# RWKV time mixing on one core: unit 1 loaded as bf16 in two halves through the casting queue, weights loaded by channel halves, and half of the second weight scaled on ScalarE

## The chip, the core and the metric

The kernel runs on one core of one Trainium2 chip. A core has a matrix engine (TensorE, PE in the profile), a vector engine (VectorE, DVE), a scalar engine (ScalarE, ACT), GpSimd (POOL) and SyncE (SP), which here only starts DMAs. Each engine works through its own instructions in order and waits on semaphores for the others. The metric is the device time of one execution in microseconds; lower is better. The median of five runs of the kernel before is 201.86 us (201.51 to 202.05).

## What is computed

Three mixes of each row of `x` with the row before it are the start of the reference; the one for `k` doesn't reach the output, and the kernel leaves it out.

```python
x_prev[:, 1:, :] = x[:, :-1, :]
xv = x * time_mix_v + x_prev * (1 - time_mix_v)
xr = x * time_mix_r + x_prev * (1 - time_mix_r)
v = xv.reshape(-1, d_model) @ value_weight
r = xr.reshape(-1, d_model) @ receptance_weight
r_sigmoid = 1.0 / (1.0 + np.exp(-r))
out = (r_sigmoid * v).reshape(-1, d_model) @ output_weight
```

`x` is 16 x 2048 x 256 in float32, each weight 256 x 256, the output has the shape of `x`.

## The kernel before

**Tiling.** The 16 x 2048 rows are cut into 64 units of 512 rows; four units make a batch row `b`. In a unit each of 128 partitions holds `UJ = 4` consecutive rows. The 256 channels are two groups `ko` of 128 (`KO = 2`). For the projections the channels must lie on the partitions, so each unit is transposed into a tile `xt` (called `xt_first` in the profile for the first two batch rows): as a rule 8 transposes on TensorE into a PSUM tile `ps_t`, and a copy by ScalarE. A slot of `xt` holds the rows with one index `j`; "previous row" is then the slot before, and a slot copy (`wrap_slots`, L431 and L432) fills the first slot of a unit.

**The algebra.** The mix is written as `time_mix * (x + c * x_prev)` with `c = 1/time_mix - 1`. The factor `time_mix` is scaled into the weights, once at the start: `w_bf[:, 0]` is the receptance weight and `w_bf[:, 1]` the value weight, each with two channel groups `ko`. The mix per unit is then a scaling (L262 on VectorE, L272 on GpSimd, or L519 on ScalarE) and an addition (L284 on VectorE). The factors are `tms` (time_mix), `c_sb` (c) and `tm_prev` (1 - time_mix); `coefficients` computes them on VectorE from a small transposed tile (L174 to L187).

**Unit by unit.** For each unit `g`: the receptance projection (4 matmuls of 512 columns), the sigmoid on ScalarE (L539), the value projection (4 matmuls), the product on VectorE (L585), 8 output matmuls (L316), a copy by ScalarE (L350) and a store by SP. Between them stand the mixes of the next units and the transposes of units some way ahead. The order on each engine is the order in which the program issues the instructions: it is written out by hand (`manual_schedule`), and waits come from the tiles.

**The start.** This is where the change lies. TensorE warms up on zeros. Meanwhile:

- SP loads, in this order: unit 0 as float32 into `x_unit[:, 0]`, in two halves of two rows each, the second half (`h = 1`) first; the receptance weight into `w_f32[:, 0]`; unit 1 as float32 into `x_unit[:, 1]`, by halves; the value weight into `w_f32[:, 1]` (L130, L136, L140). In the profile `x_unit` has the name `o_sb`, from its pool.
- GpSimd makes the DMAs that cast from float32 to bf16 on the way. The first ones bring unit 2 and unit 3 into `x_first` (L149); a one-column copy ahead of them (L147) reads the loaded receptance weight and writes into `x_first`, so that the casts are issued only after that weight has landed. Behind them come the output weight (L150), four units of batch row 1 (L108) and, later, whole batch rows (L114).
- TensorE transposes unit 0 as float32 (L234), with the coefficients' transpose in between, and ScalarE copies it out (L239, L243).
- VectorE computes the coefficients, `tms`, `tm_prev`, then `c_sb`; then it scales the receptance weight to `w_prev` (two instructions, L459) and the first channel group to `w_bf[:, 0, 0]` (L466). ScalarE scales the second, `w_bf[:, 0, 1]` (L469). VectorE then makes unit 0's value mix and scales both channel groups of the value weight (L475).
- Unit 0's receptance is projected without a mix, from `xt` and shifted `xt`, with `w_prev` and `w_bf[:, 0]` (`project_unmixed`, L306), in two output halves `mo`. Between the two stand unit 1's transposes, from float32 (L210, called by `advance(1)`), with their two copies by ScalarE (L220). The first sigmoid follows.

These are the lines around that point, in the order in which they are issued:

```python
project_unmixed(ps_r, 0)
advance(1)
project_unmixed(ps_r, 1)
wrap_slots(pieces(1)[0])
scale(pieces(1)[0])
last = add(pieces(1)[0])
```

Of the kernel before, what the change touches and what calls it, by code (L numbers as in the profile page):

```python
# [8 lines left out]
FP32 = mybir.dt.float32  # L9
BF16 = mybir.dt.bfloat16  # L10
ALU = mybir.AluOpType
ACT = mybir.ActivationFunctionType
# [3 lines left out]
def kernel(  # L16
# [38 lines left out]
    H = UJ // 2  # L55
# [11 lines left out]
    consts = ctx.enter_context(tc.tile_pool(name="consts", bufs=1))  # L67
# [4 lines left out]
    opool = ctx.enter_context(tc.tile_pool(name="opool", bufs=3))  # L72
    ps_t_pool = ctx.enter_context(tc.tile_pool(name="ps_t", bufs=2, space=bass.MemoryType.PSUM))
# [9 lines left out]
    x_bf = {}  # L83
    xt = {}
    mix = {}
    o_sb = {}
# [4 lines left out]
    ident_f = consts.tile([P, P], FP32)  # L91
    make_identity(nc, ident_f)
    ident = consts.tile([P, P], BF16)
# [5 lines left out]
    def unit_rows(t, b, e, n=1):  # L99

        return t[b, e * TU : (e + n) * TU, :].rearrange("(e p j) d -> p e j d", p=P, j=UJ)
# [15 lines left out]
            for j in (0, J // 2)  # L117
        ]

    x_unit = opool.tile([P, 2, UJ, D], FP32, name="o_sb")  # L120
    tm_rows = consts.tile([2 * KO, P], FP32)
    w_f32 = consts.tile([P, 2, KO, D], FP32)
    for m, tm in enumerate([time_mix_r, time_mix_v]):
        nc.scalar.dma_start(
            out=tm_rows[m * KO : (m + 1) * KO, :], in_=tm.rearrange("(ko p) -> ko p", p=P)
        )

    def load_halves(e):
        for h in (1, 0):
            nc.sync.dma_start(  # L130
                out=x_unit[:, e, h * H : (h + 1) * H],
                in_=unit_rows(x, 0, e)[:, 0, h * H : (h + 1) * H, :],
            )

    load_halves(0)
    nc.sync.dma_start(  # L136
        out=w_f32[:, 0], in_=receptance_weight.rearrange("(ko p) n -> p ko n", p=P)
    )
    load_halves(1)
    nc.sync.dma_start(out=w_f32[:, 1], in_=value_weight.rearrange("(ko p) n -> p ko n", p=P))  # L140
    sig0 = consts.tile([P, 1], BF16)
    nc.scalar.activation(out=sig0, in_=zeros[:, 0:1], func=ACT.Sigmoid)
    w_bf = consts.tile([P, 2, KO, D], BF16)
    w_prev = consts.tile([P, KO, D], BF16)
    wo_bf = consts.tile([P, KO, D], BF16)
    x_first = consts.tile([P, 2, UJ, D], BF16)
    nc.gpsimd.tensor_copy(out=x_first[:, 0, 0, 0:1], in_=w_f32[:, 0, 0, 0:1])  # L147
    for e in (2, 3):
        nc.gpsimd.dma_start(out=x_first[:, e - 2], in_=unit_rows(x, 0, e)[:, 0])  # L149
# [22 lines left out]
    def coefficients():  # L172
        ps = ps_o_pool.tile([P, 2, KO], FP32, name="psum_o")
        nc.tensor.transpose(  # L174
            out=ps.rearrange("p m k -> p (m k)"), in_=tm_rows, identity=ident_f[: 2 * KO, : 2 * KO]
        )
        tm = consts.tile([P, 2, KO], FP32)
        nc.vector.tensor_copy(out=tm, in_=ps)
        nc.vector.tensor_scalar(
            out=tms, in0=tm, scalar1=0.0, scalar2=1e-30, op0=ALU.is_equal, op1=ALU.mult  # L180
        )
        nc.vector.tensor_tensor(out=tms, in0=tms, in1=tm, op=ALU.add)
        nc.vector.tensor_scalar(
            out=tm_prev, in0=tm, scalar1=-1.0, scalar2=1.0, op0=ALU.mult, op1=ALU.add
        )
# [12 lines left out]
    def transposes(i):  # L198

        b, e = divmod(i, UB)  # L200
        if b > 0 and e == 0:
            new_xt(b)
        if b >= BYUNIT:
            e = (e - 1) % UB
        j0 = 1 + e * UJ + (e if b < BYUNIT else 0)
        if b < BYUNIT or e == UB - 1:
            late_copies.append((b, e))

        def one(ps, jj, ko, src, idn):
            nc.tensor.transpose(  # L210
                out=ps[:, jj], in_=src[:, jj, ko * P : (ko + 1) * P], identity=idn
            )

        if i == 1:
            for h in (1, 0):
                ps = ps_t_pool.tile([P, H, KO, P], FP32, name="ps_t")
                for jj in range(H):
                    for ko in range(KO):
                        one(ps[:, :, ko], jj, ko, x_unit[:, i, h * H : (h + 1) * H], ident_f)
                nc.scalar.copy(out=xt[b][:, j0 + h * H : j0 + (h + 1) * H], in_=ps)  # L220
            return
        ps = ps_t_pool.tile([P, UJ, KO, P], BF16, name="ps_t")
        src = x_first[:, e - 2] if b == 0 else x_bf[b][:, e * UJ : (e + 1) * UJ, :]
        for jj in range(UJ):
            for ko in range(KO):
                one(ps[:, :, ko], jj, ko, src, ident)
        nc.scalar.copy(out=xt[b][:, j0 : j0 + UJ], in_=ps)  # L227

    def first_transposes():
        def part(lo, n, pool, name):  # L230
            ps = pool.tile([P, n, KO, P], FP32, name=name)
            for jj in range(n):
                for ko in range(KO):
                    nc.tensor.transpose(  # L234
                        out=ps[:, jj, ko],
                        in_=x_unit[:, 0, lo + jj, ko * P : (ko + 1) * P],
                        identity=ident_f,
                    )
# [20 lines left out]
    def scale(piece, kos=(0, 1)):  # L259
        b, m, _, _ = piece  # L260
        for ko in kos:
            nc.vector.tensor_scalar(  # L262
                out=mixed(piece)[:, :, ko],
                in0=xt[b][:, slots(piece), ko],
                scalar1=c_sb[:, m, ko : ko + 1],
                scalar2=None,
                op0=ALU.mult,
            )
# [189 lines left out]
    for ko in range(KO):  # L458
        nc.vector.tensor_scalar(  # L459
            out=w_prev[:, ko, :],  # L460
            in0=w_f32[:, 0, ko, :],
            scalar1=tm_prev[:, 0, ko : ko + 1],
            scalar2=None,
            op0=ALU.mult,
        )
# [3 lines left out]
    nc.scalar.activation(  # L469
        out=w_bf[:, 0, 1, :], in_=w_f32[:, 0, 1, :], func=ACT.Copy, scale=tms[:, 0, 1:2]  # L470
    )
    scale(pieces(0)[1])
    add(pieces(0)[1])
    for ko in range(KO):
        nc.vector.tensor_scalar(  # L475
            out=w_bf[:, 1, ko, :],
            in0=w_f32[:, 1, ko, :],
            scalar1=tms[:, 1, ko : ko + 1],
            scalar2=None,
            op0=ALU.mult,  # L480
        )
    warm_up(WARM2)


# [42 lines left out]
    for g in range(NU - 1):  # L527
# [106 lines left out]
```

## Time and profile before

| | |
|---|---|
| median of five runs | 201.86 us (201.51 to 202.05) |
| profiled execution | 201.84 us |
| its span, first to last instruction | 200.1 us |
| busy TensorE | 195.0 us (97%) |
| busy VectorE | 185.7 us (93%) |
| busy ScalarE | 181.0 us (90%) |
| busy GpSimd | 83.5 us (42%) |
| granted TensorE clock | 1.0 |
| read from HBM, written | 34.34 MB, 33.55 MB |

How to read it: the four compute engines are busy at the same time, and a unit takes about 3.05 us in the middle of the run (from one value projection at 45.74 us to the next at 48.79). The share of busy time is a mean over the run. In the first 20 us the picture is another one, since engines wait for first data. The loads of the start, from the view of DMA issues (KB are those that are written, the last column is the median time from issue to landing):

```profile
o_sb<-in_x_dram SPq DMA_DIRECT2D x4, 256.0 KB, 3.9
x_bf<-in_x_dram POOLq DMA_DIRECT2D x4, 256.0 KB, 7.1
x_first<-in_x_dram POOLq DMA_DIRECT2D x2, 256.0 KB, 4.2
w_f<-n_receptance_weight_dram SPq DMA_DIRECT2D x1, 256.0 KB, 4.1
w_f<-in_value_weight_dram SPq DMA_DIRECT2D x1, 256.0 KB, 5.0
wo_bf<-in_output_weight_dram POOLq DMA_DIRECT2D x1, 128.0 KB, 5.4
```

### The profile page before, as it was taken

What the parts mean: (1) busy time and instruction counts of PE and PEld (TensorE: products, weight loads), DVE (VectorE), ACT (ScalarE), POOL (GpSimd) and SP (SyncE); (2) the same over time, 40 slices, a digit from 0 to 9 for tenths busy, and PEclk for the clock granted to TensorE, in tenths of its full rate; (3) what the DMA queues carried; (4) which work ended last, traced back from release to release, by engine and by line L of the source; (5) the groups of instructions that cost most, each with busy time, mean ns of one, the idle gap of its engine ahead of it and who ended that gap; (6) DMA issues with size and microseconds to landing.
All of it is one profiled execution on the core that took longest, in us unless ns stands there. A gap on an engine that the chain in (4) does not pass through costs nothing.

```text
span 200.1 us, 3885 instructions
## 1 busy us (share of the span) xinstructions
PE 195.0 (97%) x1419; PEld 124.9 (62%) x1419; DVE 185.7 (93%) x292; ACT 181.0 (90%) x204; POOL 83.5 (42%) x115
## 2 busy tenths in 40 slices
PE   8999999999999999999999999999999999999993
PEld 7555676666666666666666666655656665655671
DVE  1899999999999999899999999999999999999982
ACT  3799899999999999999999999899999999999982
POOL 1756562452543543425443444443344444444200
PEclk9999999999999999999999999999999999999999
DMA  5899999999999999999999999999999999999675
GB/s 165 233 170 213 216 279 274 280 279 275 289 309 305 288 272 288 288 277 288 283 278 301 303 404 309 313 189 208 291 263 406 356 205 244 416 421 414 277 310 214
DMA packets 32442, 57.00 MB, mean 285 GB/s; under 512 B 21796, under 2 KB 23080, under 8 KB 28456
## 3 DMA queue, kind: packets, MB, share of 16 engines
q1 hardware_dynamic: 28208, 40.24, 58.6%
q0 software_dynamic: 4064, 16.39, 40.9%
q8 instruction: 11, 0.18, 0.3%
q10 hardware_dynamic: 152, 0.13, 0.2%
q14 instruction: 7, 0.06, 0.1%
HBM read 34.34 MB, written 33.55 MB: 339 GB/s over the span
## 4 chain that ended last, share of the span: by engine, by line
PE 85%; DVE 7%; issue 3%; ACT 2%; POOL 1%; DVEq 0%
PE psum_v L292 25%; PE psum_o L316 24%; PE psum_r L292 24%; PE ps_t L210 8%; DVE z_sb L585 2%; DVE mix L284 2%; DVE mix L262 2%; PE ps_t L156 1%; PE ps_t L316 1%; PE psum_r L306 1%; ACT mix L519 1%; ACT s_sb L539 1%; ACT xt L227 1%; PE psum_r L234 0%; PE ps_t L292 0%
## 5 line engine op out<-in xcount | busy, mean ns | idle before, releaser
L272 POOL TENSOR_SCALAR mix<-xt,c_sb 128x1024 bf16<-128x1024 bf16 (+1 forms) x55 | 61.0, 1109 | 93.0 <-DVE mix L284 84.5
L585 DVE TENSOR_TENSOR z_sb<-s_sb,psum_v 128x1024 bf16<-128x1024 bf16 (+1 forms) x64 | 76.7, 1199 | 3.1 <-PE psum_v L292 1.4
L284 DVE TENSOR_TENSOR mix<-mix,xt 128x1024 bf16<-128x1024 bf16 x112 | 77.6, 702 | 1.9 <-DVE mix L262 0.5
L292 PEld LDWEIGHTS <-w_bf 128*128 128x128 bf16 x516 | 48.7, 98 | 38.7 <-DVE mix L284 0.9
L539 ACT ACTIVATE s_sb<-psum_r 128x1024 bf16<-128x1024 f32 x63 | 65.3, 1037 | 3.7 <-PE psum_r L292 2.7
L350 ACT COPY o_sb<-psum_o 128x1024 f32<-128x1024 f32 x60 | 61.5, 1025 | 6.8 <-PE psum_o L316 6.7
L292 PE MATMUL psum_v<-mix,w_bf 128*128 128x512 bf16 (+1 forms) x256 | 65.3, 377 | 0.2
L292 PE MATMUL psum_r<-mix,w_bf 128*128 128x512 bf16 (+1 forms) x252 | 64.3, 377 | 0.2
L316 PE MATMUL psum_o<-wo_bf,z_sb 128*128 128x256 bf16 x486 | 63.2, 272 | 0.0
L316 PEld LDWEIGHTS <-z_sb 128*128 128x128 bf16 x512 | 49.8, 98 | 20.4 <-issue 1.4
L227 ACT COPY xt<-ps_t 128x1024 bf16<-128x1024 bf16 x36 | 36.9, 1040 | 0.0
L210 PEld LDWEIGHTS <-x_bf 128*128 128x128 bf16 x320 | 20.9, 98 | 8.7 <-DMA x_bf<-in_x_dram 0.4
L210 PE MATMUL ps_t<-ident,x_bf 128*128 128x128 bf16 x320 | 23.9, 219 | 0.0
L262 DVE TENSOR_SCALAR mix<-xt,c_sb 128x1024 bf16<-128x1024 bf16 (+1 forms) x49 | 22.1, 459 | 0.0
L519 ACT ACTIVATE mix<-xt,c_sb 128x1024 bf16<-128x1024 bf16 x12 | 13.9, 1156 | 0.0
L284 DVE TENSOR_TENSOR mix<-mix,xt_first 128x1024 bf16<-128x1024 bf16 x15 | 10.6, 715 | 0.1
L114 POOL DMA_DIRECT2D x_bf<-in_x_dram x13 | 8.6, 662 | 0.0
L262 DVE TENSOR_SCALAR mix<-xt_first,c_sb 128x512 bf16<-128x512 bf16 x21 | 6.4, 354 | 0.2
L227 ACT COPY xt_first<-ps_t 128x1024 bf16<-128x1024 bf16 x6 | 6.2, 1026 | 0.0
L272 POOL TENSOR_SCALAR mix<-xt_first,c_sb 128x512 bf16<-128x512 bf16 x6 | 4.1, 684 | 1.0 <-ACT mix L519 0.5
L156 PE MATMUL ps_t<-zeros 128*128 128x128 bf16 x30 | 3.2, 292 | 1.0 <-DVE zeros L90 1.0
L432 POOL COPY xt_first<-xt_first 128x254 bf16<-128x254 bf16 x5 | 2.0, 393 | 5.3 <-DVE mix L284 5.3
(70 smaller groups left out, 51.0 us busy)
## 6 DMA issues: line engine op xcount, KB each, us to landing
out_dram<-o_sb SPq DMA_DIRECT2D x28, 1024.0 KB, 14.9
x_bf<-in_x_dram POOLq DMA_DIRECT2D x13, 1024.0 KB, 24.9
out_dram<-o_sb SPq DMA_DIRECT2D x4, 512.0 KB, 3.0
out_dram<-o_sb SPq DMA_DIRECT2D x6, 256.0 KB, 2.5
o_sb<-in_x_dram SPq DMA_DIRECT2D x4, 256.0 KB, 3.9
x_bf<-in_x_dram POOLq DMA_DIRECT2D x4, 256.0 KB, 7.1
x_bf<-in_x_dram POOLq DMA_DIRECT2D x2, 512.0 KB, 11.4
x_first<-in_x_dram POOLq DMA_DIRECT2D x2, 256.0 KB, 4.2
```

What stands on the lines that cost most here:

```text
L114: return nc.gpsimd.dma_start(out=x_bf[b], in_=rows(b), max_dma_last_dim=run)
L210: nc.tensor.transpose(out=ps[:, jj], in_=src[:, jj, ko * P : (ko + 1) * P], identity=idn)
L227: nc.scalar.copy(out=xt[b][:, j0 : j0 + UJ], in_=ps)
L262: nc.vector.tensor_scalar(out=mixed(piece)[:, :, ko], in0=xt[b][:, slots(piece), ko], scalar1=c_sb[:, m, ko : ko + 1], scalar2=None, op0=A ...
L272: op = nc.gpsimd.tensor_scalar(out=mixed(piece)[:, :, 1], in0=xt[b][:, slots(piece), 1], scalar1=c_sb[:, m, 1:2], scalar2=1.0, op0=ALU.mul ...
L284: return nc.vector.tensor_tensor(out=mixed(piece), in0=mixed(piece), in1=xt[b][:, slots(piece, 1)], op=ALU.add)
L292: nc.tensor.matmul(out=ps[:, mo, :], lhsT=w_bf[:, m, ko, mo * P : (mo + 1) * P], rhs=mixed((b, m, e * TU + lo, e * TU + hi))[:, :, ko], st ...
L316: nc.tensor.matmul(out=ps[:, slot, :], lhsT=z[:, ko, jj * P : (jj + 1) * P], rhs=wo_bf[:, ko, :], start=(ko == 0), stop=(ko == KO - 1),)
L350: nc.scalar.copy(out=o_sb[b][:, j0 : j0 + UJ, :], in_=ps)
L519: nc.scalar.activation(out=mixed(piece)[:, :, ko], in_=xt[b][:, slots(piece), ko], func=ACT.Copy, scale=c_sb[:, m, ko : ko + 1],)
L539: nc.scalar.activation(out=s_sb, in_=ps_r, func=ACT.Sigmoid)
L585: nc.vector.tensor_tensor(out=z_sb[:, :, c : c + n], in0=s_sb[:, :, c : c + n], in1=ps_v[:, :, c : c + n], op=ALU.mult,)
```

## The change

- Unit 1 no longer goes through SP as float32. It is loaded by GpSimd's casting DMAs into `x_first[:, 0]` as bf16, in two halves, the second half first; `x_first` now has units 1 to 3. Its transposes are bf16, with the bf16 identity, in two PSUM tiles of half the size as before, each followed by a copy by ScalarE. `x_unit` holds only unit 0.
- The gate ahead of the casts reads unit 0's first loaded half instead of the receptance weight.
- Each weight is loaded with two DMAs, one for each channel group, receptance first, then value.
- `c_sb` (reciprocal and -1) is computed on VectorE behind the scalings of the receptance weight instead of ahead of them.
- ScalarE scales the second channel group of both weights, one right after the other; VectorE scales only the first group of the value weight.

```diff
-    x_unit = opool.tile([P, 2, UJ, D], FP32, name="o_sb")
+    x_unit = opool.tile([P, UJ, D], FP32, name="o_sb")
...
-    load_halves(0)
-    nc.sync.dma_start(
-        out=w_f32[:, 0], in_=receptance_weight.rearrange("(ko p) n -> p ko n", p=P)
-    )
-    load_halves(1)
-    nc.sync.dma_start(out=w_f32[:, 1], in_=value_weight.rearrange("(ko p) n -> p ko n", p=P))
+    halves = [slice(H, UJ), slice(0, H)]
+    for h in halves:
+        nc.sync.dma_start(out=x_unit[:, h], in_=unit_rows(x, 0, 0)[:, 0, h, :])
+    for m, weight in enumerate([receptance_weight, value_weight]):
+        for ko in range(KO):
+            nc.sync.dma_start(out=w_f32[:, m, ko], in_=weight[ko * P : (ko + 1) * P, :])
...
-    x_first = consts.tile([P, 2, UJ, D], BF16)
-    nc.gpsimd.tensor_copy(out=x_first[:, 0, 0, 0:1], in_=w_f32[:, 0, 0, 0:1])
-    for e in (2, 3):
-        nc.gpsimd.dma_start(out=x_first[:, e - 2], in_=unit_rows(x, 0, e)[:, 0])
+    x_first = consts.tile([P, UB - 1, UJ, D], BF16)
+    nc.gpsimd.tensor_copy(out=x_first[:, 0, H, 0:1], in_=x_unit[:, H, 0:1])
+    for h in halves:
+        nc.gpsimd.dma_start(out=x_first[:, 0, h], in_=unit_rows(x, 0, 1)[:, 0, h, :])
+    for e in range(2, UB):
+        nc.gpsimd.dma_start(out=x_first[:, e - 1], in_=unit_rows(x, 0, e)[:, 0])
...
-        nc.vector.reciprocal(c_sb, tms)
-        nc.vector.tensor_scalar(out=c_sb, in0=c_sb, scalar1=-1.0, scalar2=None, op0=ALU.add)
...
-        if i == 1:
-            for h in (1, 0):
-                ps = ps_t_pool.tile([P, H, KO, P], FP32, name="ps_t")
...
+        src = x_first[:, e - 1] if b == 0 else x_bf[b][:, e * UJ : (e + 1) * UJ, :]
+        for h in halves if i == 1 else [slice(0, UJ)]:
+            n = h.stop - h.start
+            ps = ps_t_pool.tile([P, n, KO, P], BF16, name="ps_t")
...
-    nc.scalar.activation(
-        out=w_bf[:, 0, 1, :], in_=w_f32[:, 0, 1, :], func=ACT.Copy, scale=tms[:, 0, 1:2]
-    )
+    for m in range(2):
+        nc.scalar.activation(
+            out=w_bf[:, m, 1, :], in_=w_f32[:, m, 1, :], func=ACT.Copy, scale=tms[:, m, 1:2]
+        )
+    nc.vector.reciprocal(c_sb, tms)
+    nc.vector.tensor_scalar(out=c_sb, in0=c_sb, scalar1=-1.0, scalar2=None, op0=ALU.add)
     scale(pieces(0)[1])
     add(pieces(0)[1])
-    for ko in range(KO):
-        nc.vector.tensor_scalar(
-            out=w_bf[:, 1, ko, :],
...
+    nc.vector.tensor_scalar(
+        out=w_bf[:, 1, 0, :], in0=w_f32[:, 1, 0, :], scalar1=tms[:, 1, 0:1], scalar2=None, op0=ALU.mult
+    )
     warm_up(WARM2)
```

More of the change, by code (lines that the diff above doesn't have):

```diff
@@ L126 @@
         )
-    def load_halves(e):
-        for h in (1, 0):
-            nc.sync.dma_start(
-                out=x_unit[:, e, h * H : (h + 1) * H],
-                in_=unit_rows(x, 0, e)[:, 0, h * H : (h + 1) * H, :],
-            )
-    load_halves(0)
-    nc.sync.dma_start(
-        out=w_f32[:, 0], in_=receptance_weight.rearrange("(ko p) n -> p ko n", p=P)
-    )
-    load_halves(1)
-    nc.sync.dma_start(out=w_f32[:, 1], in_=value_weight.rearrange("(ko p) n -> p ko n", p=P))
+    halves = [slice(H, UJ), slice(0, H)]
[4 more added lines that the diff above has]
+            nc.sync.dma_start(out=w_f32[:, m, ko], in_=weight[ko * P : (ko + 1) * P, :])
     sig0 = consts.tile([P, 1], BF16)
@@ L207, in transposes @@
             late_copies.append((b, e))
[L209 to L212, printed above, removed]
-        if i == 1:
-            for h in (1, 0):
-                ps = ps_t_pool.tile([P, H, KO, P], FP32, name="ps_t")
-                for jj in range(H):
-                    for ko in range(KO):
[L219 to L227, printed above, removed]
+        src = x_first[:, e - 1] if b == 0 else x_bf[b][:, e * UJ : (e + 1) * UJ, :]
+        for h in halves if i == 1 else [slice(0, UJ)]:
+            n = h.stop - h.start
+            ps = ps_t_pool.tile([P, n, KO, P], BF16, name="ps_t")
+            for jj in range(n):
+                for ko in range(KO):
+                    nc.tensor.transpose(
+                        out=ps[:, jj, ko],
+                        in_=src[:, h.start + jj, ko * P : (ko + 1) * P],
+                        identity=ident,
+                    )
+            nc.scalar.copy(out=xt[b][:, j0 + h.start : j0 + h.stop], in_=ps)
     def first_transposes():
@@ L235, in part @@
                         out=ps[:, jj, ko],
-                        in_=x_unit[:, 0, lo + jj, ko * P : (ko + 1) * P],
+                        in_=x_unit[:, lo + jj, ko * P : (ko + 1) * P],
                         identity=ident_f,
@@ L468 @@
     )
-    nc.scalar.activation(
-        out=w_bf[:, 0, 1, :], in_=w_f32[:, 0, 1, :], func=ACT.Copy, scale=tms[:, 0, 1:2]
-    )
+    for m in range(2):
[4 more added lines that the diff above has]
+    nc.vector.tensor_scalar(out=c_sb, in0=c_sb, scalar1=-1.0, scalar2=None, op0=ALU.add)
     scale(pieces(0)[1])
     add(pieces(0)[1])
-    for ko in range(KO):
-        nc.vector.tensor_scalar(
-            out=w_bf[:, 1, ko, :],
[L477 to L481, printed above, removed]
+    nc.vector.tensor_scalar(
+        out=w_bf[:, 1, 0, :], in0=w_f32[:, 1, 0, :], scalar1=tms[:, 1, 0:1], scalar2=None, op0=ALU.mult
+    )
     warm_up(WARM2)
```

## The prediction

> **What bounds the kernel now.** I read the page first (TensorE 97% busy, and the chain that ended last is 85% TensorE), then that chain in order of time, because the change only touches the first dozen microseconds and the question is what decides there. The chain of waits over the whole run has these links; the columns are start, length, engine, written tile, line:
>
> ```profile
> 6.28 1.02 PE psum_r L306 x4
> 7.30 0.97 PE ps_t L210 x8
> 8.27 0.88 PE psum_r L306 x4
> ...
> 10.09 0.72 ACT mix L519
> 10.93 0.69 POOL mix L272
> ...
> 12.71 0.88 DVE mix L262 x3
> ...
> 19.39 1.04 PE psum_v L292 x4
> ```
>
> The reader is to see that unit 0's receptance projection (L306, two column halves `mo`), with unit 1's transposes (L210) between the halves, leads to the sigmoid at 9.17, then ScalarE's scaling L519, GpSimd's L272, its next DMA issue and slot copy, and so to VectorE's L262 at 12.71. VectorE is the longest link until 19.39; TensorE takes over there. Behind that the chain is compute again, with no transfer in it, so a shift at 9.17 that reaches 12.71 comes out at the end.
>
> The timeline of the first 13 us shows what stands around this link (start, length, engine, line, operation; in brackets idle time before, and what ended it):
>
> ```profile
> 7.77 1.12 ACT L220 CAST xt_first<-ps_t 128x512 bf16<-128x512 f32 x2 [1.14 <-PE ps_t L210]
> 9.17 1.02 ACT L539 ACTIVATE s_sb<-psum_r 128x1024 bf16<-128x1024 f32 x1 [0.28 <-PE psum_r L306]
> ...
> 5.74 0.62 DVE L459 TENSOR_SCALAR w_prev<-w_f,tm_prev 128x256 bf16<-128x256 f32 x2
> 8.20 0.74 DVE L475 TENSOR_SCALAR w_bf<-w_f,tms 128x256 bf16<-128x256 f32 x2 [0.32 <-DMA w_f<-in_value_weight_dram]
> 9.24 0.76 DVE L262 TENSOR_SCALAR mix<-xt_first,c_sb 128x512 bf16<-128x512 bf16 x2
> ...
> 5.77 0.19 POOL L147 CAST x_first<-w_f 128x1 bf16<-128x1 f32 x1 [4.46 <-DMA w_f<-n_receptance_weight_dram]
> 6.27 1.28 POOL L149 DMA_DIRECT2D x_first<-in_x_dram  x2 [0.31 <-POOL x_first L147]
> ```
>
> ScalarE has an idle 1.14 us, VectorE one wait of 0.32, and GpSimd stands 4.46 us at the gate. The stretches show what the transfers do (last two columns: DMA share and GB/s):
>
> ```profile
> 1.75:3.25 1.50, 1.50 (x17) 1.50 (x16) 0.00 (x0) 1.32 (x2) 0.00 (x0) 1.00 0.87 318
> 3.25:4.75 1.50, 1.50 (x10) 1.04 (x7) 0.00 (x0) 0.12 (x1) 0.00 (x0) 1.00 0.77 169
> 4.75:6.75 2.00, 1.93 (x15) 1.44 (x15) 1.83 (x10) 1.84 (x5) 0.67 (x2) 1.00 1.03 376
> 6.75:7.75 1.00, 1.00 (x8) 0.69 (x8) 0.97 (x3) 0.00 (x0) 1.00 (x3) 1.00 0.26 90
> 7.75:10.25 2.50, 2.43 (x16) 1.24 (x16) 2.04 (x8) 2.20 (x4) 2.50 (x5) 1.00 1.04 184
> ```
>
> The DMA engines are almost idle between 6.75 and 7.75, when the plain loads are done and the casts, issued at 6.27, haven't begun. The casts then run at 184 GB/s (written bytes): a cast of 256 KB of bf16 is 1.42 us of the queue.
>
> The DMA view, asked one issue at a time, gives landings: unit 0's first half 0.74 + 2.6 = 3.34; the receptance weight 1.66 + 4.1 = 5.77; the value weight 3.14 + 5.0 = 8.14; the first cast 6.27 + 3.7 = 9.97; the second 7.0 + 4.8 = 11.8.
>
> **The change, part by part.** The span is 200.1 us, the profiled execution 201.84, so 1.7 us lie around the span; the median of the five runs is 201.86, and shifts are put on that.
>
> *The gate and the casts.* The gate now waits for the landing at 3.34. From gate copy to first issue was 0.50 (5.77 to 6.27), so the first issue stands at 3.9. GpSimd then issues nine DMAs where it issued seven: by the rows 0.74 for the first, 0.54 for each further x_first, 0.71 for the output weight, 2.18 for four x_bf, done at 9.15 instead of 10.42. Its next work, L272, waits for ScalarE until 10.93, so this hides. The fourth x_bf issue gets a new wait for the first half's landing; GpSimd reaches it near 8.6, after that landing, so it costs nothing. The two halves together are the bytes of the first cast of before, which took 3.7 us from issue: second half at 3.9 + 3.7 = 7.6, first half 0.71 earlier, 6.9. Before had that row on nearly idle engines; now the value weight (262 KB, at 376 GB/s 0.70 us) is in the other queue at the same time. If it all goes first, the second half lands at 8.3. If the fixed part is as in the plain load of unit 0's first half (2.6 us less some 0.75 of data at 318 to 390 GB/s, 1.85) it is 3.9 + 1.85 + 1.42 = 7.2. I take 7.6 plus half of the 0.70, 7.95, since both queues have work at once; ends 7.2 and 8.3.
>
> *TensorE.* Eight float transposes (0.97 on the chain) go; eight bf16 ones, 0.61 in unit 2's row, come. Its order stays: half `mo` 0, transposes, half `mo` 1, so whatever is late in the cast stands in front of the second half. That half ends at landing + 0.07 (to the first weight load) + 0.31 (four transposes) + 0.88 = 9.21, against 9.15: +0.06. Break-even is a landing at 7.89. The best that can be had is transposes straight behind `mo` 0 (7.2): 7.2 + 0.61 + 0.88 = 8.69, a gain of 0.46.
>
> *ScalarE.* It gets one more weight scaling, 0.51 by L469. It fits into the idle 1.14 if the value weight's second half is there; otherwise the two copies of unit 1 (1.12) queue behind it, and behind them the sigmoid. In its queue the value weight follows the receptance weight directly, since unit 1 has left: earliest 5.77 + 0.70 = 6.47; latest, if both cast halves pass between, 7.9. I take the middle, 7.2: scaling done 7.74, copies can start, TensorE's second half of transposes ends 8.33, copies done 8.9, as before (8.89). Sigmoid not held. Break-even for this wait: 9.15 - 1.12 - 0.51, some 7.5.
>
> A rule stands against this part. The Trainium skill, DMA: Bandwidth & Descriptors, section SWDGE vs HWDGE vs iDMA, says that an engine takes turns between its software and its hardware queue. The trace has no stretch in this phase in which both were full, since the old gate kept them apart. By the rule in its strict form both late ends hold, +0.41; by its absence the early ones.
>
> *VectorE.* The order is now: weights first, then reciprocal and -1 (0.32, moved, not removed), one weight scaling of 0.37 less, and no 0.32 wait if the value weight's first half is there by 7.9. Start to start by the rows: `w_prev` 5.48 if the receptance weight's first half has landed by then, + 0.55 + 0.26 + 0.32 + 0.64 + 0.69 + 0.37 + 0.38 = 8.69 for unit 1's L262, against 9.24; 9.0 if both halves land at 5.77. It then waits for ScalarE's copies, 8.9: a gain of 0.2 to 0.3. But its next steps need GpSimd's L272 (11.62) and slot copy before L262 at 12.71, which follow the sigmoid. So the gain is turned into a wait on GpSimd, and counts only as far as the sigmoid moves.
>
> *The rest.* Unit 2's, unit 3's, the output weight's and x_bf's data come earlier: the cast queue starts 2.35 us earlier and carries 1.42 more. TensorE's waits for them (0.53 for unit 3, 0.4 for x_bf) vanish, but they lie beside VectorE's stretch up to 19.39; if that cover went, they'd be worth these 0.9. SP issues six loads in both. Later loads wait for the same earlier casts as before.
>
> Sum: sigmoid +0.06, all else covered: 201.86 + 0.06 = 201.92.
>
> **The rivals.** *Faster:* the cast lands by 7.5 and the value weight by 7.1. For it: the fixed part of the plain loads (7.2) and the idle 6.75 to 7.75 that goes. Against: the cast row is the nearer one. The gain is capped at 0.46 by `mo` 0 and the transposes: 201.40. The Trainium skill, DMA: Bandwidth & Descriptors, section Anatomy of one DMA, gives an estimate of 2.0 us plus bytes/436 GB/s; with 0.6 us for the 256 KB it would land at 6.5, and the sum would be this cap.
>
> *Slower, by the value weight:* ScalarE is in order, and the scaling of `w_bf[:, 1, 1]` stands ahead of unit 1's copies. Landing at 7.9 gives copies until 9.56, sigmoid 9.58 instead of 9.17: +0.41, 202.27; it decides from 7.5 on, one for one. For it: this weight landed 5.0 us after its issue; against: it then had 512 KB more ahead of it.
>
> *Slower, by the cast:* the second cast of before needs 5.53 us from the first issue for 2.84 us of data, a fixed part of 2.69 instead of 2.28. With that, and half of the value weight, the second half lands at 8.36: +0.47, 202.33; it decides from 7.89 on.
>
> *It doesn't do what it says:* the receptance weight's halves both land at 5.77, and VectorE wins nothing; the time is that of the forecast, since the sigmoid decides.
>
> **How the numbers follow.** A measurement of this kernel can tell about 0.2%, 0.4 us, from no change (five runs span 0.54). Forecast (between -0.4 and +0.4): 0.42, 201.92. Faster: 0.20. Value weight late: 0.22; cast late: 0.16. Bounds add a slow tail at the late side: both late ends with another 0.4 give 202.7. Range 201.4 to 202.7; the forecast's own is 201.5 to 202.25. Faster 0.20, same 0.42, slower 0.38.
>
> **What would show it.** In the changed profile: GpSimd's gate copy near 3.4 and first cast at 3.9; unit 1's last transposes at 8.0 to 8.35; sigmoid between 8.8 and 9.6; ScalarE's second weight scaling, with a DMA ahead of it if the value weight is late; VectorE waiting for GpSimd near 11.6 if its gain is lost as said. Wrong would be: a sigmoid earlier by over 0.4 with an unchanged end, or an unchanged sigmoid with a changed end; then something behind 12 us decides that I have put at nothing.

## The result and the profile after

| | before | after |
|---|---|---|
| median | 201.95 us (201.45 to 203.7) | 202.71 us (202.06 to 203.28) |
| profiled execution | 201.84 us | 203.04 us |
| its span | 200.1 us | 201.2 us |

The ratio after to before is 1.0034, with a 95% interval of 1.0026 to 1.0043: the change makes the kernel slower by 0.34%, some 0.7 us, which is more than the 0.2% that can be told from no change. (The 201.95 is the median of 79 runs of the kernel before, taken beside the 44 of the changed one; the prediction counts from the first five, 201.86.) The profiled execution after lies 0.33 us above its median, the one before 0.11 below, so the two profiled executions are further apart than the medians (1.2 us).

The chain of waits after, from 4.6 us on (start, length, engine, tile, line):

```profile
4.63 4.83 DMA x_first<-in_x_dram
9.46 0.05 issue
9.51 0.40 PE ps_t L208 x4
9.90 0.88 PE psum_r L292 x4
10.78 0.02 issue
10.80 1.03 ACT s_sb L523
11.84 0.02 issue
11.86 0.63 DVE z_sb L569
...
13.93 0.88 DVE mix L248 x3
...
20.61 1.04 PE psum_v L278 x4
```

Before, the chain of these microseconds was compute; now the first link shown is a transfer of 4.83 us, the second half of unit 1. It lands at 9.46. Behind it the order of the chain is as it was, later by a constant: VectorE's L248 x3 (L262 before) at 13.93 instead of 12.71, TensorE's `psum_v` at 20.61 instead of 19.39, both +1.22. At the end 1.2 are left.

The timeline of the same stretch (idle time and what ended it in brackets):

```profile
6.13 0.91 ACT L456 ACTIVATE w_bf<-w_f,tms 128x256 bf16<-128x256 f32 x2
...
9.94 0.59 ACT L213 COPY xt_first<-ps_t 128x512 bf16<-128x512 bf16 x1 [1.42 <-PE ps_t L208]
...
8.70 0.21 DVE L418 COPY xt_first<-xt_first 128x254 bf16<-128x254 bf16 x1
10.56 0.62 DVE L248 TENSOR_SCALAR mix<-xt_first,c_sb 128x512 bf16<-128x512 bf16 x2 [1.65 <-ACT xt_first L213]
...
3.92 1.25 POOL L142 DMA_DIRECT2D x_first<-in_x_dram  x2 [0.31 <-POOL x_first L140]
5.15 1.09 POOL L144 DMA_DIRECT2D x_first<-in_x_dram  x2
...
12.10 0.69 POOL L258 TENSOR_SCALAR mix<-xt_first,c_sb 128x512 bf16<-128x512 bf16 x1 [2.97 <-DVE mix L270]
...
9.51 0.40 PE L208 MATMUL ps_t<-ident,x_first 128*128 128x128 bf16 x4 [1.61 <-DMA x_first<-in_x_dram]
```

TensorE waits 1.61 us for the transfer, ScalarE's second copy 1.42 for TensorE, VectorE 1.65 for ScalarE: one late landing seen from three engines. ScalarE's two weight scalings run without a wait at 6.13, so the value weight is not late.

The DMA view, one issue at a time (KB written, last column from issue to landing): unit 2, issued at 5.15 (256 KB), and unit 1's second half, issued at 4.63 (128 KB).

```profile
x_first<-in_x_dram POOLq DMA_DIRECT2D x1, 256.0 KB, 6.1
x_first<-in_x_dram POOLq DMA_DIRECT2D x1, 128.0 KB, 4.8
```

Before, the first cast took 3.7 us for 256 KB; here half of that takes 4.8, and unit 2, issued 1.1 us earlier than before, lands at 11.27 instead of 9.93. The stretches show why it isn't a matter of bytes (last two columns: DMA share, GB/s):

```profile
4.75:5.75 1.00, 1.00 (x7) 0.90 (x7) 0.82 (x5) 1.00 (x3) 1.00 (x3) 1.00 0.72 214
5.75:6.75 1.00, 0.95 (x11) 0.59 (x10) 0.96 (x5) 0.94 (x4) 1.00 (x2) 1.00 1.12 153
6.75:8.25 1.50, 0.95 (x7) 0.31 (x5) 1.36 (x4) 0.61 (x2) 1.50 (x4) 1.00 1.09 76
8.25:9.50 1.25, 0.00 (x0) 0.00 (x0) 0.67 (x4) 0.27 (x1) 0.88 (x2) 1.00 0.99 148
```

Between 6.75 and 8.25 the sixteen engines are counted as busy throughout (1.09; the view counts a packet whole in the stretch in which it begins) and yet move 76 GB/s, less than half of the 184 GB/s at which the casts ran before. In the records of single packets, nine of unit 2's first twelve, which begin between 6.78 and 7.85, take 0.9 to 2.0 us each, and four of unit 1's from 6.55 on 0.7 to 1.0; the usual times are 0.17 and 0.10 (unit 2's packets write 2 KB, those of unit 1's halves 1 KB). The plain loads' packets are all through by 5.8, so this is not the value weight taking turns with the cast.

### The profile page after: what moved, and what is told of

The parts are those of the page before. It is cut to its first block, busy times and chain, and to the rows that moved or that the text cites. A ratio compares the mean times of both kernels' runs of the same rounds, so it can differ in the third digit from the quotient of the medians.

```text
span 201.2 us, 3886 instructions
## 1 busy us (share of the span) xinstructions
PE 194.4 (97%) x1419; PEld 124.8 (62%) x1419; DVE 185.3 (92%) x291; ACT 181.2 (90%) x205; POOL 84.6 (42%) x117
## 4 chain that ended last, share of the span: by engine, by line
PE 82%; DVE 7%; DMA 4%; issue 3%; ACT 2%; POOL 0%; DVEq 0%
PE psum_v L278 25%; PE psum_o L302 24%; PE psum_r L278 23%; PE ps_t L208 8%; DVE z_sb L569 3%; DMA x_first<-in_x_dram 2%; DVE mix L270 2%; DVE mix L248 2%; DMA o_sb<-in_x_dram 1%; PE ps_t L302 1%; ACT s_sb L523 1%; ACT mix L503 1%; ACT xt L213 1%; PE psum_r L292 0%; PE ps_t L278 0%
## 5 line engine op out<-in xcount | busy, mean ns | idle before, releaser
L270 DVE TENSOR_TENSOR mix<-mix,xt 128x1024 bf16<-128x1024 bf16 x112 | 77.1, 697 | 1.9 <-DVE mix L248 0.5
L248 DVE TENSOR_SCALAR mix<-xt,c_sb 128x1024 bf16<-128x1024 bf16 (+1 forms) x49 | 22.1, 459 | 0.0
L270 DVE TENSOR_TENSOR mix<-mix,xt_first 128x1024 bf16<-128x1024 bf16 x15 | 10.6, 714 | 0.1
L213 ACT COPY xt_first<-ps_t 128x1024 bf16<-128x1024 bf16 (+1 forms) x8 | 7.3, 918 | 2.3 <-PE ps_t L208 2.3
L248 DVE TENSOR_SCALAR mix<-xt_first,c_sb 128x512 bf16<-128x512 bf16 x21 | 6.3, 348 | 1.9 <-ACT xt_first L213 1.6
```

The lines of the kernel that those rows point to most:

```text
L213: nc.scalar.copy(out=xt[b][:, j0 + h.start : j0 + h.stop], in_=ps)
L248: nc.vector.tensor_scalar(out=mixed(piece)[:, :, ko], in0=xt[b][:, slots(piece), ko], scalar1=c_sb[:, m, ko : ko + 1], scalar2=None, op0=A ...
L270: return nc.vector.tensor_tensor(out=mixed(piece), in0=mixed(piece), in1=xt[b][:, slots(piece, 1)], op=ALU.add)
```

## The experiments

In all of them four numbers were read: when unit 2's cast is issued, when the last of unit 1 and unit 2 land, and when VectorE's second product begins (L585 of before, unit 1's). The last is the best short measure of the loss: it is at 14.11 before and 15.33 after. "Long" counts the packets of more than 0.6 us between 4.8 and 12.8 us, with the longest. The ratios are from 6 to 44 runs each; everything right of them is of one profiled execution.

| kernel | ratio (95%) | unit 2 issued | unit 1 landed | unit 2 landed | long | second product | span |
|---|---|---|---|---|---|---|---|
| before | 1 | 6.27 | 7.51 | 9.93 | 1 (0.68) | 14.11 | 200.1 |
| after | 1.0034 (1.0026–1.0043) | 5.15 | 9.46 | 11.27 | 17 (2.00) | 15.33 | 201.2 |
| e1_second_gate | 1.0104 (1.0071–1.0137) | 8.66 | 8.06 | 12.26 | 0 | 15.81 | 201.9 |
| e2_cast_only | 1.0039 (1.0018–1.0060) | 5.22 | 8.68 | 11.21 | 13 (1.66) | 14.69 | 200.8 |
| e3_unit1_by_sp | 1.0062 (1.0037–1.0086) | 5.88 | 8.47 | 12.20 | 11 (1.31) | 15.76 | 202.1 |
| e4_quiet_vector | one time, 202.97 us | 5.13 | 8.67 | 11.72 | 15 (2.06) | 15.20 | 201.2 |
| e5_gate_behind_units | 1.0051 (1.0027–1.0076) | 5.19 | 8.55 | 11.36 | 16 (1.75) | 15.08 | 201.5 |
| e6_one_cast | 1.0028 (1.0004–1.0052) | 4.70 | 8.90 | 10.47 | 20 (1.28) | 15.28 | 201.2 |
| e7_gate_on_value | 0.9995 (0.9969–1.0021) | 6.68 | 8.13 | 10.40 | 1 (0.64) | 14.04 | 200.0 |
| e8_before_again | one time, 201.78 us | 6.20 | 7.54 | 9.88 | 0 | 14.04 | 200.0 |
| e9_gate_on_ident | 1.0118 (1.0075–1.0161) | 9.52 | 8.71 | 13.12 | 0 | 16.67 | 202.7 |
| e10_all_by_halves | 1.0028 (1.0005–1.0051) | 5.21 | 9.59 | 11.05 | 11 (1.98) | 15.45 | 201.4 |
| e11_gate_on_receptance | 1.0069 (1.0052–1.0086) | 5.92 | 8.42 | 11.94 | 17 (1.08) | 15.49 | 201.5 |
| e12_gate_behind_unit2 | 1.0035 (1.0012–1.0057) | 5.17 | 9.21 | 10.55 | 18 (1.67) | 15.07 | 201.0 |

The second product and the span go together over all fourteen traces, within 0.6 us (from 14.04 and 200.0 to 16.67 and 202.7): nearly all of the loss is made ahead of the second product, and nothing behind gives it back. One landing is not exact to a tenth: in the six traces in which unit 1's halves are cast with unit 2 straight behind (after, e2, e4, e5, e10, e12), the last of unit 1 lands anywhere from 8.55 to 9.59.

### Which part of the change, and is it what follows the cast?

**e1_second_gate:** the changed kernel, with units 2 and 3 issued only when unit 1 has landed.

```diff
     for h in halves:
         nc.gpsimd.dma_start(out=x_first[:, 0, h], in_=unit_rows(x, 0, 1)[:, 0, h, :])
+    nc.gpsimd.tensor_copy(out=x_first[:, 1, 0, 0:1], in_=x_first[:, 0, 0, 0:1])
     for e in range(2, UB):
```

> The changed kernel with a second gate: GpSimd issues the casts of units 2 and 3 and all that is behind them only after the first half that is loaded last (unit 1, rows 0 and 1) has landed. In the changed kernel that half landed at 9.46 us, 4.8 us after its issue, while units 2 and 3 were in the same queue behind it and GpSimd was issuing more. Theory 'what is issued behind it slows it': the second half lands by 7.6 to 8.0, the sigmoid is at 9.2 or earlier. Rival 'an early cast is slow by itself, or is starved by other engines': it lands at 9 or later again. In both the data of unit 2 comes late (landing of unit 1 plus 0.5 plus 3.7 us), so the time says less than the landing: with the theory some 202.5 to 203.5, with the rival 204 to 205.

The gate copy shows the landing directly:

```profile
8.12 0.25 POOL L143 COPY x_first<-x_first 128x1 bf16<-128x1 bf16 x1 [2.99 <-DMA x_first<-in_x_dram]
```

The half lands at 8.06, 1.4 us earlier than in the changed kernel, and no packet is long. So what is issued behind unit 1 is what makes it late. The time is worse all the same: unit 2 now lands at 12.26, and TensorE waits 1.13 us for it. The time can't price the earlier landing, and the sigmoid isn't at 9.2 either but at 10.44, with the first product at 11.85, since this execution was late ahead of unit 1: unit 0's second half landed at 5.27 instead of 4.47, and the first projections began at 6.97 instead of 6.29, with 1.06 us for a pair of matmuls that takes 0.59 in the changed kernel.

**e2_cast_only:** the kernel before, with unit 1 cast by halves behind the early gate, and nothing else of the change: weights whole, in the old order, and scaled as before.

> The kernel before with one part of the change alone: unit 1 as bf16 by halves through the casting queue, gated on unit 0's first half. The weights are loaded whole and scaled as before. Theory 'the whole loss is the landing of unit 1': sigmoid at 10.5 or later, 0.5 to 1.2 us slower than before, as the changed kernel. Rival 'the weights' halves or ScalarE's second scaling make the loss': within 0.3 us of before.

Its ratio, 1.0039, is that of the whole change. Unit 1 lands at 8.68 and unit 2 at 11.21, with thirteen packets of 0.60 to 1.66 us. The loss comes with the cast; it needs neither the weights by channel halves nor the moved reciprocal nor ScalarE's extra scaling. (What these are worth by themselves, some 0.2% either way, the two intervals don't tell.)

**e3_unit1_by_sp:** the reverse, everything but the cast of unit 1. Unit 1 goes as float32 through SP, behind the four weight halves, and the casts start with unit 2, gated on the receptance weight's second half.

```diff
+    load_halves(0)
+    load_weight(0, receptance_weight)
+    load_weight(1, value_weight)
+    load_halves(1)
...
+    nc.gpsimd.tensor_copy(out=x_first[:, 0, 0, 0:1], in_=w_f32[:, 0, 1, 0:1])
+    for e in (2, 3):
+        nc.gpsimd.dma_start(out=x_first[:, e - 2], in_=unit_rows(x, 0, e)[:, 0])
```

> The changed kernel with the cast of unit 1 undone: unit 1 goes through SP as float32 by halves, behind the four weight loads, and the other casts wait for the receptance weight's second half. The weights by halves, ScalarE's second scaling and the later reciprocal stay. Theory 'the whole loss is the landing of unit 1 through the casting queue': unit 1 lands at 7.4 to 8.1, sigmoid 9.1 to 9.6, time within 0.4 us of before (201.6 to 202.35). Rival 'the other parts cost the time': 0.5 us or more slower, with the sigmoid at 10 or later.

Both accounts missed: 1.0062 is slower than either said. Unit 2's cast, the first in its queue and issued at 5.88, takes 6.3 us, where the first cast of the kernel before, issued at 6.27, took 3.7. TensorE then waits for it:

```profile
12.34 0.61 PE L210 MATMUL ps_t<-ident,x_first 128*128 128x128 bf16 x8 [1.38 <-POOL xt_first L431]
```

The line names GpSimd, but these transposes need unit 2's data, which landed at 12.20, and not the slot copy: in the changed kernel the same transposes run at 11.47, ahead of the slot copy at 12.75. And four of unit 1's plain packets are long here too, 0.63 to 1.31 us from 5.37 on; three of them begin before 5.88, when no cast had been issued at all. So long packets are not a matter of the cast queue alone. (Part of the 6.3 us may be unit 2's turns with unit 1's plain packets, which run until 8.09; the run doesn't separate the two.)

### What in the following casts?

**e4_quiet_vector:** the changed kernel with VectorE's mix of unit 0 (L248 and L270) moved behind unit 1's copies, which leaves VectorE idle while the casts move.

```diff
-    scale(pieces(0)[1])
-    add(pieces(0)[1])
...
             advance(1)
+            scale(pieces(0)[1])
+            add(pieces(0)[1])
```

> The changed kernel, with VectorE's mix of unit 0 (two scalings and an addition, 7.06 to 8.40 us in the changed kernel) moved behind the copies of unit 1, so that VectorE is idle from some 7.3 us until unit 1 has landed. Theory 'VectorE's work holds up GpSimd's casts': the second half of unit 1 lands by 8.0. Rival 'VectorE has nothing to do with it': it lands at 9.2 to 9.7 again. The kernel is slower than the changed one if the landing stays, since the mix then comes later (up to 1.2 us).

VectorE stands still from 7.13 to 8.50, and five packets that begin in that time still take 0.77 to 2.06 us. The landing, 8.67, lies between the two values that were expected, nearer the rival's, and within the spread of the landings above; the packets decide: VectorE's mix is not the cause. (Its weight scalings up to 7.13 ran here as well, so they are not excluded.)

**e5_gate_behind_units:** a second gate behind the casts of units 2 and 3, so that GpSimd issues nothing more until unit 1 is there.

```diff
     for e in range(2, UB):
         nc.gpsimd.dma_start(out=x_first[:, e - 1], in_=unit_rows(x, 0, e)[:, 0])
+    nc.gpsimd.tensor_copy(out=wo_bf[:, 0, 0:1], in_=x_first[:, 0, 0, 0:1])
```

> The changed kernel with the second gate behind the casts of units 2 and 3: only the output weight and batch row 1 wait until unit 1 has landed. With the gate ahead of units 2 and 3 unit 1's second half landed at 8.06 us and no packet ahead of 8.1 us took over 0.6 us; without it the landings were 8.67 to 9.46. Theory 'units 2 and 3, whose packets are in the same engines behind it, slow it': lands at 8.6 or later again, with packets of unit 2 of over 1 us. Rival 'GpSimd's further issuing (output weight and batch row 1, 6.2 to 9.1 us) slows it': lands by 8.2, no packets over 0.7 us. Time: some 202.3 to 203.3 with the first; with the second 201.5 to 202.3, if the later data doesn't hold up anything.

Unit 1 lands at 8.55 and packets take up to 1.75 us: GpSimd's further issuing isn't what slows them.

**e6_one_cast** takes the halves away, **e10_all_by_halves** makes halves of everything.

```diff
-    for h in halves:
-        nc.gpsimd.dma_start(out=x_first[:, 0, h], in_=unit_rows(x, 0, 1)[:, 0, h, :])
-    for e in range(2, UB):
+    for e in range(1, UB):
         nc.gpsimd.dma_start(out=x_first[:, e - 1], in_=unit_rows(x, 0, e)[:, 0])
```

```diff
     for e in range(2, UB):
-        nc.gpsimd.dma_start(out=x_first[:, e - 1], in_=unit_rows(x, 0, e)[:, 0])
+        for h in halves:
+            nc.gpsimd.dma_start(out=x_first[:, e - 1, h], in_=unit_rows(x, 0, e)[:, 0, h, :])
```

> The changed kernel with unit 1 as one cast in place of two halves, so that all of the first packets are of one size. Theory 'the halves, with packets of half size and one more DMA, are what slows the queue': unit 1 lands at 7.6 to 8.0, as 3.7 us from the issue in the kernel before, and unit 2 has no long first packets; time 201.5 to 202.3. Rival 'the early casts behind each other are slow whatever their size': lands at 8.5 or later, time as the changed kernel (202.3 to 203.1).

> The changed kernel with units 2 and 3 cast by halves as well and no second gate: every early packet then reads 2 KB and writes 1 KB. In the changed kernel it was the first packets of unit 2 (2 KB written) that took 1 to 2 us; with unit 1 as one cast it was unit 1's own. Theory 'the packets of double size are what blocks': no packet over 0.7 us, unit 1 lands by 8.2, time 201.8 to 202.3. Rival 'whatever follows unit 1 so early blocks': landing at 8.6 or later, time as the changed kernel (202.3 to 203.1).

As one cast, unit 1 lands at 8.90, and its own packets from 5.5 on are among the long ones. With everything in halves it lands at 9.59, with packets of half the size at up to 1.98 us. Neither the halves nor the packet size is the cause.

### When may the following casts be issued?

**e7_gate_on_value:** the changed kernel with a second gate ahead of units 2 and 3 that reads the last half of the value weight.

```diff
         nc.gpsimd.dma_start(out=x_first[:, 0, h], in_=unit_rows(x, 0, 1)[:, 0, h, :])
+    nc.gpsimd.tensor_copy(out=x_first[:, 1, 0, 0:1], in_=w_f32[:, 1, 1, 0:1])
     for e in range(2, UB):
```

> The changed kernel with the second gate on the landing of the value weight's second half (6.05 us in the changed kernel) in place of unit 1's: units 2 and 3 are issued at 6.6 instead of 5.15, near the 6.27 of the kernel before. Theory 'what is behind unit 1 in the queue slows it': unit 1 lands at 8.0 to 8.2, since its packets are nearly through at 7.5 to 8.1 when unit 2's begin; sigmoid at 9.2 to 9.4; time within 0.3 us of the kernel before (201.5 to 202.1). Rival 'long first packets come whenever casts run in this stretch': unit 2's first packets are long again and the time is 202.3 or more.

One instruction undoes the loss (ratio 0.9995). The timeline:

```profile
6.16 0.22 POOL L143 CAST x_first<-w_f 128x1 bf16<-128x1 f32 x1 [1.03 <-DMA w_f<-in_value_weight_dram]
6.68 1.05 POOL L145 DMA_DIRECT2D x_first<-in_x_dram  x2 [0.30 <-POOL x_first L143]
...
10.84 0.69 POOL L259 TENSOR_SCALAR mix<-xt_first,c_sb 128x512 bf16<-128x512 bf16 x1 [0.23 <-DVE mix L271]
...
9.23 0.69 DVE L249 TENSOR_SCALAR mix<-xt_first,c_sb 128x512 bf16<-128x512 bf16 x2 [0.34 <-ACT xt_first L214]
9.96 0.69 DVE L271 TENSOR_TENSOR mix<-mix,xt_first 128x1024 bf16<-128x1024 bf16 x1
10.56 1.22 DVE L570 TENSOR_TENSOR z_sb<-s_sb,psum_v 128x1024 bf16<-128x1024 bf16 x1
...
9.48 1.02 ACT L524 ACTIVATE s_sb<-psum_r 128x1024 bf16<-128x1024 f32 x1 [0.28 <-PE psum_r L293]
10.40 0.71 ACT L504 ACTIVATE mix<-xt_first,c_sb 128x512 bf16<-128x512 bf16 x1
```

Unit 2 is issued 1.5 us later than in the changed kernel and lands 0.9 earlier (10.40, 3.7 us from issue), and unit 1 lands at 8.13. Its stretch from 6.75 to 8.25 moves about the same number of bytes as the changed kernel's, at a DMA share of 0.66 instead of 1.09:

```profile
6.75:8.25 1.50, 1.20 (x10) 0.44 (x9) 1.47 (x4) 0.46 (x2) 1.50 (x3) 1.00 0.66 85
```

**e8_before_again**, the kernel before, unchanged, stands beside it:

> The kernel before, unchanged, for a second profile: in the first one the cast of unit 2 had no packet over 0.4 us and landed 3.7 us after its issue. If the long packets of the changed kernel belong to its order, the second profile has none either (landing of unit 2 at 9.6 to 10.2); if they are chance, it may have them.

```profile
9.18 0.76 DVE L262 TENSOR_SCALAR mix<-xt_first,c_sb 128x512 bf16<-128x512 bf16 x2
...
10.58 1.21 DVE L585 TENSOR_TENSOR z_sb<-s_sb,psum_v 128x1024 bf16<-128x1024 bf16 x1
```

It has no long packet, and unit 2 lands at 9.88: the long ones belong to the changed order. Unit 1's scaling is at 9.18 there and 9.23 in e7, the product at 10.58 and 10.56: a cast that isn't disturbed brings unit 1 into the mix at the same moment as the float32 load did.

**e9_gate_on_ident:** e7 with the first gate on the identity matrix, so that unit 1's casts are issued at 2.12 and 2.83, beside the weights.

```diff
-    nc.gpsimd.tensor_copy(out=x_first[:, 0, H, 0:1], in_=x_unit[:, H, 0:1])
+    nc.gpsimd.tensor_copy(out=x_first[:, 0, H, 0:1], in_=ident[:, 0:1])
```

> The kernel with the second gate on the value weight, and the first gate moved ahead: unit 1's casts wait for the bf16 identity (ready at 1.57 us) instead of unit 0's first half (3.34), so they are issued near 2.1 and their packets begin near 3.6, beside the weights. Theory 'unit 1's landing sets VectorE's next scaling, and an earlier one passes through to the end': unit 1 lands by 6.5 to 7.2, VectorE's scaling of unit 1 at 8.7 to 9.0 (9.23 with the later gate), sigmoid near 8.75, time 0.2 to 0.5 us below before (201.35 to 201.75). Rival 'the casts take the weights' place': receptance weight at 5.8 or later, unit 0's second half late, and the time at before or up to 0.5 us above.

The casts take the weights' place, and more than the rival said (ratio 1.0118). The DMA view of e9, with 3.3 us for the receptance weight in the changed kernel:

```profile
w_f<-n_receptance_weight_dram SPq DMA_DIRECT2D x2, 128.0 KB, 5.0
x_first<-in_x_dram POOLq DMA_DIRECT2D x2, 128.0 KB, 5.7
```

The receptance halves land at 6.32 and 7.50 instead of 4.98 and 5.33, and `w_prev` waits 0.91 and 0.76 us for them. So two queues do share the engines here, as the Trainium skill, DMA: Bandwidth & Descriptors, section SWDGE vs HWDGE vs iDMA, says. Between 4.8 and 12.8 us no packet is long in this run: here the sharing costs later landings without long packets, and is a different thing from what befalls the changed kernel.

The late weights are not all of this run's loss. TensorE waits for `w_prev` (0.91 and 0.72 us), and after that its granted clock in the profiled execution is half for 3.4 us (third column from the end):

```profile
8.25:11.75 3.50, 3.50 (x16) 1.83 (x16) 3.10 (x10) 1.58 (x3) 2.42 (x5) 0.51 0.31 43
```

The other thirteen traces have no record of a clock below full in their first 16 us (the records begin between 3.8 and 9.2 us). A pair of the 512-column matmuls takes 1.00 to 1.06 us in this stretch, and 0.59 in the changed kernel. Half of the 3.4 us, 1.7, is an upper estimate of what this costs, of the 2.4 us that the run loses.

**e11_gate_on_receptance:** the second gate on the receptance weight's second half, so that unit 2 is issued at 5.92.

```diff
+    nc.gpsimd.tensor_copy(out=x_first[:, 1, 0, 0:1], in_=w_f32[:, 0, 1, 0:1])
     for e in range(2, UB):
```

> The changed kernel with the second gate (ahead of the casts of units 2 and 3) on the receptance weight's second half, which landed at 5.33: these casts are issued about 0.7 to 0.9 us later than in the changed kernel (near 5.9 to 6.1 instead of 5.15), 0.6 to 0.8 earlier than with the gate on the value weight (6.7). Theory (it is how soon the next cast follows, by degrees): unit 1's second half lands between 8.3 and 9.2, unit 2 at 10.5 to 11.2, the time between the two, 202.1 to 202.6. Rival (an all-or-nothing rule: any cast whose issue begins before unit 1's packets have started spoils them): the landing stays at 9.2 or later, time 202.6 or more. Second rival (only a straight run of issues counts, a gap of half a microsecond is enough): landing 8.2, time as before, 201.8 to 202.1.

Half of it came true. Unit 1 lands at 8.42, within what the theory said, and VectorE's first product is at 10.87, only 0.2 late. But unit 2 lands at 11.94, not by 11.2, and the ratio, 1.0069, is worse than without the second gate:

```profile
12.07 0.61 PE L209 MATMUL ps_t<-ident,x_first 128*128 128x128 bf16 x8 [1.49 <-POOL xt_first L418]
```

TensorE waits 1.49 us before these, unit 2's transposes. (As in e3 the named slot copy, which ends 0.04 us after the landing, is not what they need.) So there are two ways to lose by the same slow packets: unit 1 late, or unit 2 late. Issued 0.76 us earlier than in e7, unit 2 lands 1.5 later. Neither "by degrees" nor "a gap is enough" describes that.

**e12_gate_behind_unit2:** the gate of e7 one cast later, so that unit 2 alone is issued straight behind unit 1.

```diff
     for e in range(2, UB):
+        if e == 3:
+            nc.gpsimd.tensor_copy(out=x_first[:, 2, 0, 0:1], in_=w_f32[:, 1, 1, 0:1])
         nc.gpsimd.dma_start(out=x_first[:, e - 1], in_=unit_rows(x, 0, e)[:, 0])
```

> The changed kernel with the second gate, on the value weight's second half, one cast later: unit 2 is issued straight behind unit 1 at 5.15 as in the changed kernel, unit 3 and all that follows only at 6.7. Theory (the one cast that follows directly is enough): unit 2's first packets again take 0.9 us and more, unit 1's second half lands at 8.5 or later, unit 2 near 11, time 202.4 or more. Rival (it takes a deep queue: several casts outstanding when the first data move): no packet over 0.6 us, unit 1 lands near 8.1 and unit 2 at 10.0 or earlier, time 201.6 to 202.1.

The theory held: unit 1 lands at 9.21, packets take up to 1.67 us, ratio 1.0035. One cast that follows is enough; it needs no deep queue. (Unit 3, issued at 6.74, is in the queue before most of the long packets begin, but in e7 a cast issued at 6.68 brought none.)

### What is shown, and what stays open

Shown: the loss is the late landing of unit 1's second half (and, where that is mended half-way, of unit 2), it comes with packets of 0.6 to 2 us, and it goes when unit 2's cast is issued later. In the table the issue of unit 2 divides all fourteen traces: at 5.92 or earlier there are 11 to 20 long packets, at 6.20 or later none or one. Where the packets tell the units apart (1 KB for unit 1, 2 KB for unit 2), the same line shows in them: in after, e2, e4, e5, e11 and e12 unit 2's first packet begins before unit 1's last has ended (after: 6.78 and 9.13), in e1, e7 and e9 it begins behind it (e7: 8.03 and 7.86). Whether that overlap makes packets long or comes of it, the records don't say.

Not shown is why. "A cast straight behind a cast" can't be all: in the kernel before, unit 3 is issued 0.74 us behind unit 2, and no packet suffers; and in e3 unit 2 is the first cast, and plain packets suffer, three of them ahead of it. Excluded are the halves, the packet size, VectorE's mix, GpSimd's issues behind unit 3, a deep queue, and instruction fetches (in the before, after, e3, e7 and e11 traces none falls between 0 and 16 us). What the memory or the descriptors do in that time wasn't tried.

## Why the prediction was right, and where it was wrong

Put on the 201.86 from which the prediction counts, the ratio gives 202.55, inside the range of 201.4 to 202.7 and 0.6 above the mid value of 201.92; the median by itself, 202.71, is at the range's very edge. It lies outside the forecast's own 201.5 to 202.25, and the sign is the one that was given 0.38, not the likeliest. That the range holds it is in part luck: its slow end adds two late landings and another 0.4, and what came was one landing, later by up to 1.6 us than the mid value, for a reason that the prediction doesn't have.

- **The gate and the issue times** held: gate copy at 3.42, first issue at 3.92, GpSimd done at 9.13 (forecast 3.4, 3.9, 9.15).
- **The cast's landing** is the step that was mis-sized: "I take 7.6 plus half of the 0.70, 7.95", between 7.2 and 8.3, against 9.46 (8.55 to 9.59 over the six traces with that order). The prediction looked for the disturbance in the other queue, in the value weight, which was through the engines by 5.8; it came with the casts that follow. It had no price in the trace of before, where the first cast had casts behind it and kept to 3.7 us. Undisturbed, the term was well sized: 8.06 in e1 and 8.13 in e7.
- **"When the plain loads are done"** was read a little early: in the trace of before the last plain packets end at 7.83, and the 90 GB/s between 6.75 and 7.75 are theirs. The casts begin at 7.76 there, as said.
- **TensorE's order** was read rightly: what is late in the cast stands ahead of the second half `mo`, one for one from 7.89 on. By that rule a landing at 9.46 moves the sigmoid by 1.57; it moved by 1.63 (9.17 to 10.80), out of the 8.8 to 9.6 that was expected.
- **The third rival** named the mechanism (the cast late) but not its cause, and its price, 0.47, belongs to a landing at 8.36.
- **The value weight** landed at 5.75 and 6.05, earlier than the lower bound of 6.47. So the second rival, given the larger share of the slow side, never came near; e2 shows that the loss needs no change of the weights.
- **VectorE** was nearly on time: `w_prev` at 5.50 (forecast 5.48), ready for unit 1's scaling at 8.91 (forecast 8.69). "Its next steps need GpSimd's L272 (11.62) and slot copy before L262 at 12.71, which follow the sigmoid" was wrong in its last words. The chain before led through sigmoid, ScalarE's mix and L272, but L272 doesn't need that mix: in e7 and in after GpSimd's scaling starts (10.84, 12.10) while ScalarE's mix (10.40 and 11.72, for 0.71 us) is still running. In the program it waits for VectorE's addition (`scale_pool(p, last)`), and it starts 0.19 to 0.20 us behind that addition's end in all three: 10.73 and 10.93 before, 10.65 and 10.84 in e7, 11.90 and 12.10 after. The chain of before named ScalarE's mix because it ended at 10.80, 0.07 behind the addition:

```profile
10.04 0.69 DVE L284 TENSOR_TENSOR mix<-mix,xt_first 128x1024 bf16<-128x1024 bf16 x1
10.09 0.71 ACT L519 ACTIVATE mix<-xt_first,c_sb 128x512 bf16<-128x512 bf16 x1
10.93 0.69 POOL L272 TENSOR_SCALAR mix<-xt_first,c_sb 128x512 bf16<-128x512 bf16 x1 [0.51 <-ACT mix L519]
```

  That also explains how a sigmoid at 9.48 in e7 goes with a product as early as before's, and why 1.63 us at the sigmoid became only 1.22 at the product: before, the sigmoid ended at 10.19 and the product began at 10.64, so some 0.4 was slack. VectorE's scaling of unit 1, behind ScalarE's copies, sets the pace.
- **"The rest", that unit 2's data come earlier,** was wrong in sign: issued 1.1 us earlier, they land 1.3 later.
- **The step from 12.71 to the end** held: the +1.22 at the product is +1.22 at 20.61 and +1.2 at the end.

No version that was run beats the kernel before; e7 equals it. There the last of unit 1 lands at 8.13, and 9.2 us for its mix is what the float32 load gives as well.

## What to carry to other kernels

A transfer's duration is not a constant to be moved to another place of the timeline: read what is issued behind it there as well as what runs beside it. Issuing a load earlier can make it, and the one ahead of it, land later; a gate that holds back the next transfers is a cheap way to try this, and what it reads decides (of three gates straight ahead of unit 2, the one that let it go at 8.66 was too late, at 5.92 too early, at 6.68 right). Where two possible releasers end within a tenth of a microsecond of each other, the chain names the later one; which of them the instruction needs, the program says.

## What was not expected of the hardware

DMA engines that are counted as busy need not be moving much: a share of 1.09 with 76 GB/s, in single packets of up to 2.0 us where 0.17 is usual, against 0.66 with 85 GB/s in the same stretch of e7. And halving a cast hardly shortens it: in e1 and e7, with at most one long packet, those of 128 KB took 3.5 to 3.6 us from issue to landing, the first of 256 KB 3.6 to 3.7. The Trainium skill, DMA: Bandwidth & Descriptors, section Anatomy of one DMA, has a fixed part of 2.0 us; 128 KB would take 2.3 by its formula, as an estimate, and the bytes that are read, 256 KB, 2.6. Every cast of these runs took longer, so here the measurement decides.
